# Two weight groups split on VectorE, squares of x on two engines, an earlier first split, and last sums by tokens, in a one-layer diffusion trunk on one core

## The chip, the cores and the metric

The kernel runs on one core of a Trainium2 chip. The metric is device microseconds of one execution; every version gets a median of several runs. A profile is one execution of its own, read with the views of the trace. The engines go by short names: PE is TensorE (PEld its weight loads), DVE VectorE, ACT ScalarE, POOL GpSimd, and SP is SyncE, which only issues transfers. Every engine works through its own instructions in order, and the transfers that SP and POOL issue stand in those engines' order too.

## What is computed

One inference step of a backbone with one trunk layer, over 128 context tokens and 512 latent tokens with 1,024 channels. Cut to what matters here:

```python
def rmsnorm(x, g):
    xf = x.astype(jnp.float32)
    y = xf * lax.rsqrt(jnp.mean(xf * xf, axis=-1, keepdims=True) + EPS)
    return y.astype(x.dtype) * g
...
    sh1, sc1, g1, sh2, sc2, g2 = jnp.split(mod.astype(x.dtype), N_MOD, axis=-1)
    h = rmsnorm(x, p['norm1_g']) * (1 + sc1) + sh1
    proj = jnp.einsum('btd,dc->btc', h, p['w_in']) + p['b_in']
...
    q, k, v, o, i_f, f_f, i_b, f_b, u, ga, gb = jnp.split(proj, offs, axis=-1)
    hA, st_f, st_b = mlstm_bidir(...)          # four heads, forward and backward
    branch_a = jnp.einsum('bte,ed->btd', jax.nn.sigmoid(o) * hA, p['w_proj_a'])
    ua, ub = jnp.split(u, 2, axis=-1)
    z = dwconv1d(ua * jax.nn.sigmoid(ub), p['conv_dw_w'], p['conv_dw_b'])   # 31 taps
    z = jax.nn.silu(layernorm(z, p['conv_ln_g'], p['conv_ln_b']))
    branch_b = jnp.einsum('bte,ed->btd', z, p['w_proj_b'])
    merged = jax.nn.sigmoid(ga) * branch_a + jax.nn.sigmoid(gb) * branch_b
    x = x + g1 * jnp.einsum('btd,de->bte', merged, p['w_out'])
    ...                                        # second norm, gated MLP with a depthwise convolution
    y = rmsnorm(x, p['final_norm_g'])
```

`mod` comes from a linear map of the conditioning vectors. Context tokens see only context tokens.

## The kernel before

**Layout.** Channels lie on the 128 partitions and the 640 tokens are columns, so that x is eight tiles of 128x640. Both token sets go through every matmul together, in two halves of 320 columns.

**Weights in three products.** The weights come in 138 groups of eight 128x128 blocks (512 KB). A group is loaded by SP into a staging buffer `wst` (three of them) and split into a high half `wh` in a format that PE runs at full rate, and a low half `wl`, the remainder; there are three buffers for each half. The activations are split alike (`hh`, `hl`), and a product is the sum of three: `hh`·`wh`, `hl`·`wh` and `hh`·`wl`. A group of the input projection is so 8 blocks x 3 products x 2 column halves = 48 matmuls.

**Two ways to the low half** (`prep`, line 474). ACT always writes `wh`. For most groups DVE then subtracts: `wl = wst - wh`. For groups in the set `TWICE` (lines 162 to 164) ACT writes a second, negated copy into `wl`, and POOL issues a transfer that adds the group from HBM onto it once more (the accumulating DMA `wl<-in_w`), which leaves the same remainder. DVE has no part in these. `TWICE` holds input groups from the seventh on, except those that the value projections hold, and most groups of the MLP. The groups around the change are u2 (11), u6 (12), u3 (13), u7 (14), k2 (15), q2 (16), k3 (17), q3 (18), then the values v1 (19 and 20): u is the input of the gated convolution, k and q are keys and queries of a head.

**What orders the work.** The kernel is emitted once by a planner, `_Order` (line 187): each operation gets an estimated duration; side tasks are generators (`spawn`, line 288) that are advanced when the estimated time of PE has come to their inputs (`until`, line 305), and convolution taps are background work (`later`, `fill`) put in where DVE's estimate leaves a hole. `force` (line 275) runs a task to its end at once. The planner's estimates only set the order; on the chip every engine waits for what it needs.

**The start.** `colsum_into` (line 665) sums squares over the partitions: four matmuls of a 128x32 block of ones, each over a quarter of the tokens (160 columns), so that the sums lie as 128x160, each quarter repeated over 32 partitions. The squares of the eight x tiles are all on ACT (lines 725 to 732), with the tanh of the conditioning and the change to the square root's function table after the fourth. `rstd` (line 683) makes 1/sqrt with one Newton step: a square root on ACT (`rsy`), then on DVE `rsv`, a reciprocal, and three small products (`rst`, `rst`, `rsy`). `bcast` lays the result out as one row per token for all partitions. `ada1` (line 757) makes the modulation from eight columns of weights (`adst`): matmuls with `sc_pad`, a copy `mrow` on ACT, a transposing matmul, then `mods` and `a` on DVE. `first_h` multiplies x by the norm and applies the modulation, giving `hh` and `hl`. `prep(0)` splits the first weight group; it is called before `ada1` starts, and its operations go out when the planner's time for them has come.

**The masks.** In the middle, the scan's decay matrices `E` are filled: `spread` (line 1109) broadcasts rows with SP's transfers, then POOL adds a mask from HBM with accumulating transfers `E<-in_mask`, three per pair of heads. In POOL's order they stand among the accumulating transfers of the weights and the small memsets of the padded `glu` tiles for the convolution.

**The convolution.** `glu` is the gated product of a u pair (128x656 with its padding). ACT makes a first tap (`z<-glu,cols`), and DVE adds the others in 0.8 us each, `z<-glu,cols,z`, in a chain per 128 channels (m = 0 to 3).

**The end.** The last down projection is done in two parts of tokens, 384 and 256 (`PARTS`, line 1747). For each, `final` (line 1749) waits for the squares, which are added on DVE into two tiles, sums them with `colsum_into`, calls `rstd`, lays the row out with `bcast_part`, multiplies and stores. The second part's chain is the last work in the program.

Of the kernel before, what the change touches and what calls it, by code (L numbers as in the profile page):

```python
# [12 lines left out]
AF = mybir.ActivationFunctionType  # L13
ALU = mybir.AluOpType

P = 128
# [4 lines left out]
T = NCTX + NLAT  # L21
# [55 lines left out]
TL = 384  # L77
# [71 lines left out]
GB = 8  # L149
BLOCKS, HELD, PAIRS = _blocks()  # L150
# [10 lines left out]

_IN = [_g for _g in range(NGRP) if BLOCKS[_g * GB][0] in ("q", "k", "v", "u", "o")]
TWICE = set(_IN[6:]) - {_g + 3 for _g in _IN if HELD.get(_g)}
TWICE |= {_g for _g in range(NGRP) if all(nm == "up" and m % NF >= 2 or nm[:2] == "dn" for nm, k, m in BLOCKS[_g * GB:_g * GB + GB])}
UNIT_AT = {_u: _i for _i, _u in enumerate(UNITS)}

# [196 lines left out]
def tile_trunk(  # L363
# [17 lines left out]
    od = _Order()  # L381
    V, S, G, PE, Q, GQ = (_Timed(e, od, k) for e, k in ((nc.vector, "V"), (nc.scalar, "S"), (nc.gpsimd, "G"),
                                                        (nc.tensor, "PE"), (nc.sync, "Q"), (nc.gpsimd, "R")))
# [19 lines left out]
    first, last = ExitStack(), ctx.enter_context(ExitStack())  # L403
    adp = first.enter_context(tc.tile_pool(name="adp", bufs=2 * NAD1))

    def A(shape, dt=F32, name="a"):
        return ap.tile(shape, dt, tag="A", name=name)
# [18 lines left out]
    def ps():  # L426
        return od.ring("ps", pools["ps"].tile([P, 512], F32, tag="ps", name="ps"), pools["nps"])
# [2 lines left out]
        return t[:, 0:T].rearrange("p (h n) -> p h n", h=2)  # L430

    HALF = [slice(0, TH), slice(TH, T)]


    cols = cp.tile([P, NCOLS], F32, name="cols")
    sel = cp.tile([P, NSEL], F32, name="sel")
    ident = sel[:, 0:128]
# [15 lines left out]
    lines = {}  # L453
# [17 lines left out]
    def wtile(tag):  # L471
        return od.ring(tag, (wf[0] if tag == "wf" else wp).tile([P, GB * P], F32R, tag=tag, name=tag), CAPS[tag])

    def prep(g, tags=("wh", "wl")):


        if g in ready or g >= NGRP:
            return
        load(g)
        src = stage.pop(g)  # L480
        tag_of["c", g, 0] = tags
        hi, lo = wtile(tags[0]), wtile(tags[1])

        def parts():
            yield from od.until(src)
            S.activation(hi, src, AF.Copy)
            if g in TWICE:
                S.activation(lo, src, AF.Copy, scale=-1.0)
                live.pop(g)
                GQ.dma_start(lo, w_d[g], accum_op=ALU.add)  # L490
                return
            yield
            V.tensor_sub(lo, src, hi.bitcast(F32))
            live.pop(g)

        ready[g] = (hi, lo)
        lines[g] = od.spawn(parts())
# [137 lines left out]
    def mtile(mat, m, ks, xs, pt=None, first=True, last=True):  # L635
        pt = mm_ps() if pt is None else pt
        outs = [(bank(pt, h), HALF[h]) for h in range(2)]
        for i, k in enumerate(ks):
# [3 lines left out]
    def views(pt, t, rows=slice(0, P)):  # L642
# [3 lines left out]
        if isinstance(pt, tuple):  # L646
            return [(bank(pt, h)[rows], t[:, HALF[h]]) for h in range(2)]
        return [(pt[rows, :, 0:TH], halves(t))]
# [10 lines left out]
    ones32 = cp.tile([P, 32], F32, name="ones32")  # L659
    V.memset(ones32, 1.0)  # L660
    epsc = cp.tile([P, 1], F32, name="epsc")
    V.memset(epsc, EPS)
    bgrp = T // 4

    def colsum_into(pc, tile_, n, first, last):
# [4 lines left out]
    def bcast(r, n):  # L670
        out = []
        for h in range(2):
            pt = ps()
            for j in range(2):
                g = 2 * h + j
                PE.matmul(pt[:, j * n:(j + 1) * n], lhsT=sel[:, 256 + g:257 + g].to_broadcast([P, P]), rhs=r,
                          start=True, stop=True)
            out.append(pt[:, 0:2 * n])
        return out

    def rstd(src, w, scale, name):

# [17 lines left out]
    x = []  # L700
    for j in range(KD):
        t = A([P, T], name="x")
# [21 lines left out]
    pc = ps()  # L724
    for j in range(KD):
        sq = A([P, T], name="sq")
        S.activation(sq, x[j], AF.Square)
        if j == 3:
            th = small([P, 16], "th")
            S.activation(th, colr("c"), AF.Tanh, scale=0.5)  # L730
            sqrt_table()
        colsum_into(pc, sq, bgrp, j == 0, j == KD - 1)
# [11 lines left out]
    for nm in ("b_ua", "b_ub", "b_o", "mlstm_g", "ln_g", "ln_b", "b_ga", "b_gb"):  # L744
        a, b = _COLS[nm]
# [2 lines left out]
        o += b - a  # L748

    r1 = rstd(pc[:, 0:bgrp], bgrp, 1.0 / D, "rs")  # L750
    prep(0)

    def hcol(name, i):
        return halfc[:, HC[name] + i:HC[name] + i + 1]
# [31 lines left out]
    def first_h(j):  # L786
        while not rbs:
            yield
        if j == 0:
            for h in range(2):  # L790
                V.tensor_mul(x[j][:, HALF[h]], x[j][:, HALF[h]], rb[h])
        else:
# [13 lines left out]
    t_ada = od.spawn(ada1())  # L806
    while not mrows:
        od.finish_one()
    rb = bcast(r1, bgrp)
    t = A([P, T], name="rbs")  # L810
    for h in range(2):
        S.activation(t[:, HALF[h]], rb[h], AF.Copy)
    rbs.append(t)
# [130 lines left out]
    for p in range(2):  # L944
        for c in range(NCH):
            t = vp.tile([P, 2, P1], F32, tag="v", name="va")
# [437 lines left out]
    for i, (nm, m) in enumerate(BRANCH):  # L1384
# [9 lines left out]
        else:  # L1394
# [4 lines left out]
            a, b = sgt.pop(("ga", m)), sgt.pop(("gb", m))  # L1399
# [33 lines left out]
    def sums_in(sums, adds, n):  # L1433

        while not all(t[2] for t in adds):
            yield
        pc = ps()
        for i in range(2):
            yield from od.until(sums[i])
            colsum_into(pc, sums[i], n, i == 0, i == 1)  # L1440
        return pc[:, 0:n]

    def bcast_part(r):
        pt = ps()
        n = r.shape[1]
        for g in range(4):
            PE.matmul(pt[:, g * n:(g + 1) * n], lhsT=sel[:, 256 + g:257 + g].to_broadcast([P, P]), rhs=r,
                      start=True, stop=True)
        return pt[:, 0:4 * n]
# [35 lines left out]
    def norm2_part(h, j, rb):  # L1485
        s = HALF[h]
        t, hh = hf[j][:, h, :], h2[j, h]
# [39 lines left out]
    for h in range(2):  # L1527
        sums, adds = [], []
        mat, s = ("woA", "woB")[h], HALF[h]
        pts = [mhalf(mat, m, range(KD - 1), mg, s, last=False) for m in range(2 if h == 0 else 0)]  # L1530
        for m in range(8):
            if m < len(pts):
                pt = mhalf(mat, m, [KD - 1], mg[KD - 1:], s, pt=pts[m], first=False)
            else:
                pt = mhalf(mat, m, range(KD), mg, s)
# [6 lines left out]
    for i in range(2):  # L1542
        t = A([P, TF], name=f"gbuf{i}")
# [200 lines left out]

    ks = LASTF

    PARTS = [slice(0, TL), slice(TL, T)]

    def final(h, sums, adds):
        s = PARTS[h]  # L1750
        n = (s.stop - s.start) // 4
        pc = yield from sums_in(sums, adds, n)
        r3 = rstd(pc, n, 1.0 / D, "rs")
        yield
        yield from od.until(r3)
        rb = bcast_part(r3)
        if h == 0:
            for j in range(KD):
                V.scalar_tensor_tensor(x2[j][:, s], x2[j][:, s], col("final_g", j), rb, op0=ALU.mult, op1=ALU.mult)
                Q.dma_start(yT[j, :, s], x2[j][:, s])  # L1760
                yield
            return
        for j in range(0, KD, 2):
            t = A([P, 2, 4 * n], name="yo")
            for i in range(2):
                V.scalar_tensor_tensor(t[:, i, :], x2[j + i][:, s], col("final_g", j + i), rb,
                                       op0=ALU.mult, op1=ALU.mult)
            Q.dma_start(yT[j:j + 2, :, s].rearrange("j p n -> p j n"), t)
# [3 lines left out]
    for h in range(2):  # L1772
        mat, s = ("dnA", "dnB")[h], PARTS[h]
        sums, adds = [], []
        npre = NPRE if h == 0 else 0
        pts = [dn(mhalf, mat, m, ks[:-1], s, last=False) for m in range(npre)]
        for m in range(8):
# [3 lines left out]
            if m < npre:  # L1781
                pt = dn(mhalf, mat, m, ks[-1:], s, pt=pts[m], first=False)
            else:
                pt = dn(mhalf, mat, m, ks, s)
# [136 lines left out]
```

## Time and profile before

| | us |
|---|---|
| three runs | 949.36, 950.96, 951.27 |
| median | 950.96 |
| the profiled execution | 950.29 |
| its span (first to last instruction) | 948.5 |
| PE busy in the span | 914.2 (96%) |
| DVE busy | 742.1 (78%) |
| ACT busy | 531.6 (56%) |
| POOL busy | 130.6 (14%) |

In a time line, a row has its start in the span, its length, the engine, the line, the operation, the tile it writes, an arrow, what it reads, sizes, and how many instructions the row holds; the square brackets behind it give how long the engine was idle before, and what ended that. A row of windows has the start and end of the stretch, its length, the busy time and count of PE, PEld, DVE, ACT and POOL, then the clock granted to PE (1 is full), the share of the DMA engines and GB/s. A row of the transfers has the tile, the issuing queue, the count, the size and the median us from issue to landing. Every tile operation goes through one helper, so that all rows carry line 182 (183 in the changed kernel, which has one line more above it); rows are told apart by their tiles.

### The profile page before, as it was taken

To read this page: it belongs to the slowest core of one execution; us is meant where nothing else is said; L and a number is where in the kernel's file an instruction comes from. 1 tells how busy PE (TensorE), PEld (TensorE's weight loads), DVE (VectorE), ACT (ScalarE), POOL (GpSimd) and SP (SyncE) were. 2 spreads that over 40 slices of the span, in tenths; PEclk is the share of its full clock that TensorE was granted. 3 is DMA by queue.
4 is the path that set the end of the run, shared out by engine and by line. 5 is a ranking of instruction groups with operands and counts; after the bars stand their busy time and mean duration, and the time that the engine had idled before them with its cause. 6 is when DMAs were issued, how large, how long until landed. Compare 5 with 4: busy or idle time off the path is not lost.

```text
span 948.5 us, 16981 instructions
## 1 busy us (share of the span) xinstructions
PE 914.2 (96%) x6456; PEld 893.0 (94%) x6456; DVE 742.1 (78%) x1540; ACT 531.6 (56%) x995; POOL 130.6 (14%) x181
## 2 busy tenths in 40 slices
PE   5999997999999999999999999999999999999995
PEld 2899997999999999999999999999999999999995
DVE  3829777887857988889788996877778877878666
ACT  5564575267758222223478766646765666666662
POOL 0001212000000000000000112222222222222210
PEclk9999999899999999999999999999999999999998
DMA  9638939543215646667544769887888889889975
GB/s 356 264 121 170 241 96 264 129 101 89 79 46 166 202 154 196 205 204 257 172 156 133 166 143 201 169 179 169 183 171 183 174 172 183 176 175 185 206 166 150
DMA packets 65954, 164.90 MB, mean 174 GB/s; under 512 B 6864, under 2 KB 15824, under 8 KB 65872
## 3 DMA queue, kind: packets, MB, share of 16 engines
q1 hardware_dynamic: 41360, 113.20, 37.0%
q0 software_dynamic: 24512, 50.60, 31.5%
q8 instruction: 51, 0.84, 0.4%
q14 instruction: 31, 0.25, 0.1%
HBM read 151.39 MB, written 3.48 MB: 163 GB/s over the span
## 4 chain that ended last, share of the span: by engine, by line
PE 83%; DMA 6%; DVE 4%; ACT 3%; issue 2%; SPq 0%; DVEq 0%; POOLq 0%; POOL 0%; ACTq 0%
PE mm L182 64%; PE ps L182 19%; DMA wl<-in_w 2%; DMA E<-in_mask 1%; DMA rowM<-M 1%; DMA out_ocst<-cs 1%; DMA x<-in_xT 1%; ACT L182 1%; DMA E<-rowM 1%; DVE x L182 0%; ACT z L182 0%; SPq L182 0%; DVE wl L182 0%; DMA cb<-in_crow 0%; DVE bc L182 0%
## 5 line engine op out<-in xcount | busy, mean ns | idle before, releaser
L182 ACT ACTIVATE wh<-wst 128x1024 fp32r<-128x1024 f32 (+1 forms) x114 | 114.1, 1007 | 99.2 <-PE mm L182 85.9
L182 DVE SCALAR_TENSOR_TENSOR acc<-gbuf,cols,acc 128x455 f32<-128x455 f32 (+2 forms) x176 | 129.7, 740 | 14.8 <-ACT acc L182 12.4
L182 PE MATMUL mm<-hh,wl 128*128 128x320 f32 (+2 forms) x576 | 134.8, 313 | 5.6 <-DMA wl<-in_w 5.6
L182 PE MATMUL mm<-hh,wh 128*128 128x320 f32 (+2 forms) x576 | 134.3, 312 | 2.9 <-ACT hh L182 1.6
L182 PE MATMUL mm<-hl,wh 128*128 128x320 f32 (+2 forms) x576 | 134.9, 313 | 0.0
L182 DVE SCALAR_TENSOR_TENSOR z<-glu,cols,z 128x641 f32<-128x641 f32 (+14 forms) x120 | 102.4, 887 | 22.6 <-ACT z L182 21.6
L182 POOL DMA_DIRECT2D wl<-in_w x69 | 60.9, 883 | 390.3 <-ACT wl L182 225.5
L182 PEld LDWEIGHTS mm<-hh,wl 128*128 128x128 f32 x576 | 97.0, 190 | 7.1 <-DMA wl<-in_w 5.9
L182 PEld LDWEIGHTS mm<-hh,wh 128*128 128x128 f32 x576 | 97.7, 190 | 4.8 <-ACT hh L182 2.1
L182 PEld LDWEIGHTS mm<-hl,wh 128*128 128x128 f32 x576 | 97.1, 190 | 1.8 <-issue 1.3
L182 PE MATMUL mm<-h,wh 128*128 128x320 f32 x452 | 85.5, 310 | 1.4 <-ACT h L182 0.8
L182 DVE SCALAR_TENSOR_TENSOR junk<-ad,cb 128x512 bf16<-128x512 f32 x128 | 82.0, 685 | 0.0
L182 DVE TENSOR_TENSOR wl<-wst,wh 128x1024 fp32r<-128x1024 f32 x55 | 67.1, 1221 | 17.2 <-ACT wh L182 17.1
L182 PE MATMUL mm<-al,wh 128*128 128x320 f32 (+2 forms) x336 | 80.5, 309 | 0.0
L182 PE MATMUL mm<-ah,wh 128*128 128x320 f32 (+2 forms) x336 | 80.3, 309 | 0.0
L182 PE MATMUL mm<-ah,wl 128*128 128x320 f32 (+2 forms) x336 | 80.3, 308 | 0.0
L182 ACT ACTIVATE wl<-wst 128x1024 fp32r<-128x1024 f32 (+1 forms) x91 | 74.3, 840 | 4.7 <-PE mm L182 4.7
L182 PEld LDWEIGHTS mm<-h,wh 128*128 128x128 f32 x452 | 71.2, 188 | 2.7 <-DVE h L182 1.2
L182 PE MATMUL mm<-h,wl 128*128 128x320 f32 x364 | 73.1, 309 | 0.3 <-DMA wl<-in_w 0.3
L182 DVE SCALAR_TENSOR_TENSOR x<-mm,mods,x 128x128 f32<-128x128 f32 (+1 forms) x168 | 63.7, 433 | 8.1 <-PE mm L182 7.5
L182 PEld LDWEIGHTS mm<-h,wl 128*128 128x128 f32 x364 | 58.5, 188 | 0.6 <-DMA wl<-in_w 0.6
L182 PEld LDWEIGHTS mm<-ah,wh 128*128 128x128 f32 x336 | 57.2, 188 | 0.1
(249 smaller groups left out, 1930.6 us busy)
## 6 DMA issues: line engine op xcount, KB each, us to landing
wst<-in_w SPq DMA_DIRECT2D x138, 512.0 KB, 4.5
wl<-in_w POOLq DMA_DIRECT2D x47, 512.0 KB, 7.2
ad<-in_ada SPq DMA_DIRECT2D x64, 256.0 KB, 3.1
adst<-in_ada SPq DMA_DIRECT2D x16, 512.0 KB, 10.2
wf<-in_w POOLq DMA_DIRECT2D x23, 256.0 KB, 5.0
wh<-sf POOLq DMA_DIRECT2D x22, 256.0 KB, 5.3
wl<-in_w POOLq DMA_DIRECT2D x22, 256.0 KB, 6.0
x<-in_xT SPq DMA_DIRECT2D x16, 320.0 KB, 5.8
```

The lines of the kernel that those rows point to most:

```text
L182: return fn(*args, **kw)
```

## The change

It has four parts.

1. Groups k2 and q2 are taken out of `TWICE`: their low halves come from DVE's subtraction, and ACT's second copy and POOL's transfer for them go away.
2. The squares of x tiles 3, 4, 5 and 7 are made on DVE, those of 0, 1, 2 and 6 on ACT; the tanh and the table change come after the third tile's step.
3. `prep(0)` is called after the first `mrow`, doesn't ask the planner to wait for the load, and is forced out at once, ahead of the broadcast of the norm.
4. In the last norm's second part (256 tokens) the sums go by tokens: the squares are the weights and one column of ones is moved, so that the sums lie as 128x2, one token per partition; `rstd` works on 128x2; and `token_rows` broadcasts that column as the weight and moves an identity matrix, which gives the rows for all partitions. It is also written so that the first of the two tiles of squares can be summed before the last square is done.

```diff
 TWICE = set(_IN[6:]) - {_g + 3 for _g in _IN if HELD.get(_g)}
+TWICE -= {_g for _g in _IN if BLOCKS[_g * GB][0] in ("k", "q") and BLOCKS[_g * GB][2] == 2}
...
-    def prep(g, tags=("wh", "wl")):
+    def prep(g, tags=("wh", "wl"), wait=True):
...
-            yield from od.until(src)
+            if wait:
+                yield from od.until(src)
             S.activation(hi, src, AF.Copy)
...
+    def token_sums(pc, tile_, w, first, last):
+
+        n = w // P
+        for c in range(n):
+            PE.matmul(pc[:, c:c + 1], lhsT=tile_[:, c * P:(c + 1) * P], rhs=ones32[:, 0:1], start=first and c == 0,
+                      stop=last and c == n - 1)
+
+    def token_rows(r, a, b):
+
+        pt = ps()
+        for c in range(a, b):
+            PE.matmul(pt[:, (c - a) * P:(c - a + 1) * P], lhsT=r[:, c:c + 1].to_broadcast([P, P]), rhs=ident,
+                      start=True, stop=True)
+        return pt[:, 0:(b - a) * P]
...
         sq = A([P, T], name="sq")
-        S.activation(sq, x[j], AF.Square)
-        if j == 3:
+        if j in (3, 4, 5, 7):
+            V.tensor_mul(sq, x[j], x[j])
+        else:
+            S.activation(sq, x[j], AF.Square)
+        if j == 2:
...
     r1 = rstd(pc[:, 0:bgrp], bgrp, 1.0 / D, "rs")
-    prep(0)
...
         od.finish_one()
+    prep(0, wait=False)
+    od.force(lines[0])
     rb = bcast(r1, bgrp)
...
-        n = (s.stop - s.start) // 4
-        pc = yield from sums_in(sums, adds, n)
+        if h == 0:
+            n = (s.stop - s.start) // 4
+            pc = yield from sums_in(sums, adds, n)
+        else:
+            n = (s.stop - s.start) // P
+            while not all(t[2] for t in adds[:-1]):
+                yield
+            yield from od.until(sums[0])
+            pc = ps()
+            token_sums(pc, sums[0], n * P, True, False)
+            while not adds[-1][2]:
+                yield
+            yield from od.until(sums[1])
+            token_sums(pc, sums[1], n * P, False, True)
+            pc = pc[:, 0:n]
         r3 = rstd(pc, n, 1.0 / D, "rs")
         yield
         yield from od.until(r3)
-        rb = bcast_part(r3)
+        rb = bcast_part(r3) if h == 0 else token_rows(r3, 0, n)
```

Since the planner sets the order, the change also moves instructions. On DVE at the start, the sequence from the first norm's `rsv` on stands like this in the kernel before (a row is an operation with its output, inputs and shape, and how many of it follow one another):

```order
L182 TENSOR_SCALAR rsv<-ps 128x160
L182 RECIPROCAL rsy<-rsy 128x160
L182 TENSOR_TENSOR rst<-rsy 128x160
L182 SCALAR_TENSOR_TENSOR rst<-rst,rsv 128x160
L182 SCALAR_TENSOR_TENSOR rsy<-rst,rsy 128x160
L182 TENSOR_SCALAR mods<-ps,cols 128x2
L182 TENSOR_SCALAR a_213<-ps,sc1p,cols 128x2
L182 TENSOR_TENSOR x<-x,ps 128x320 x2
L182 TENSOR_TENSOR wl<-wst,wh 128x1024
```

In the changed kernel the same place on DVE reads:

```order
L183 RECIPROCAL rsy<-rsy 128x160
L183 TENSOR_TENSOR rst<-rsy 128x160
L183 SCALAR_TENSOR_TENSOR rst<-rst,rsv 128x160
L183 SCALAR_TENSOR_TENSOR rsy<-rst,rsy 128x160
L183 TENSOR_TENSOR wl<-wst,wh 128x1024
L183 TENSOR_SCALAR mods<-ps,cols 128x2
L183 TENSOR_SCALAR a_211<-ps,sc1p,cols 128x2
L183 TENSOR_TENSOR x<-x,ps 128x320 x2
```

The split of group 0 has moved from behind the first multiplies by the norm to between the norm's last product and `mods`. Further up, DVE's four squares (`sq<-x`) stand ahead of its small preparations of the modulation; on ACT the copy `wh` of group 0 stands ahead of `rbs`, where it stood behind.

On DVE in the middle, at the gating product `glu` of the third channel block (m = 2) and the convolution taps `z` around it, the kernel before has:

```order
L182 SCALAR_TENSOR_TENSOR z<-glu,cols,z 128x651
L182 SCALAR_TENSOR_TENSOR glu<-gt,gy 128x128
L182 SCALAR_TENSOR_TENSOR glu<-gt,gy 128x512
L182 SCALAR_TENSOR_TENSOR z<-glu,cols,z 128x652
L182 SCALAR_TENSOR_TENSOR z<-glu,cols,z 128x653
L182 SCALAR_TENSOR_TENSOR z<-glu,cols,z 128x641
L182 SCALAR_TENSOR_TENSOR z<-glu,cols,z 128x654
L182 SCALAR_TENSOR_TENSOR z<-glu,cols,z 128x642
L182 SCALAR_TENSOR_TENSOR z<-glu,cols,z 128x655
```

In the changed kernel the same place has the two new splits, k2's first and then q2's:

```order
L183 SCALAR_TENSOR_TENSOR glu<-gt,gy 128x128
L183 SCALAR_TENSOR_TENSOR glu<-gt,gy 128x512
L183 TENSOR_TENSOR wl<-wst,wh 128x1024
L183 SCALAR_TENSOR_TENSOR z<-glu,cols,z 128x652
L183 SCALAR_TENSOR_TENSOR z<-glu,cols,z 128x653
L183 SCALAR_TENSOR_TENSOR z<-glu,cols,z 128x641
L183 SCALAR_TENSOR_TENSOR z<-glu,cols,z 128x654
L183 SCALAR_TENSOR_TENSOR z<-glu,cols,z 128x642
L183 TENSOR_TENSOR wl<-wst,wh 128x1024
L183 SCALAR_TENSOR_TENSOR z<-glu,cols,z 128x655
```

One split stands right behind `glu`, the other behind five more taps (of these, 652 and 653 end the chain of the second channel block and 641 begins the third's). Some 45 rows on, the first value rows `va<-mm,vb` stand two taps earlier in the fourth block's chain than before.

On POOL, the same stretch, from the masks `E` of the second pair of heads on, reads in the kernel before:

```order
L182 DMA E<-in_mask 128x4x128
L182 DMA E_1676<-in_mask 128x8x128
L182 DMA E_1684<-in_mask 128x8x128
L182 MEMSET glu 128x15
L182 MEMSET glu 128x1
L182 DMA wl<-in_w 128x1024 x2
L182 MEMSET glu 128x15
L182 MEMSET glu 128x1
L182 DMA wl<-in_w 128x1024 x7
```

In the changed kernel:

```order
L183 DMA E<-in_mask 128x4x128
L183 DMA E_1676<-in_mask 128x8x128
L183 DMA E_1684<-in_mask 128x8x128
L183 MEMSET glu 128x15
L183 MEMSET glu 128x1
L183 MEMSET glu 128x15
L183 MEMSET glu 128x1
L183 DMA wl<-in_w 128x1024 x7
```

The two weight transfers between the memsets, those of k2 and q2, are gone, and the first that follows the masks is k3's. On PE the last rows of the program are now two sums of two 128x1 matmuls and two 128x128 matmuls for the broadcast, where two sums of four 32x64 matmuls and four of 128x64 stood.

More of the change, by code (lines that the diff above doesn't have):

```diff
@@ L432, in tile_trunk @@
     HALF = [slice(0, TH), slice(TH, T)]
+    PARTS = [slice(0, TL), slice(TL, T)]
     cols = cp.tile([P, NCOLS], F32, name="cols")
@@ L1745, in tile_trunk @@
     ks = LASTF
-    PARTS = [slice(0, TL), slice(TL, T)]
     def final(h, sums, adds):
         s = PARTS[h]
-        n = (s.stop - s.start) // 4
-        pc = yield from sums_in(sums, adds, n)
+        if h == 0:
[13 more added lines that the diff above has]
+            pc = pc[:, 0:n]
         r3 = rstd(pc, n, 1.0 / D, "rs")
@@ L1763, in final @@
         for j in range(0, KD, 2):
-            t = A([P, 2, 4 * n], name="yo")
+            t = A([P, 2, n * P], name="yo")
             for i in range(2):
```

## The prediction

> **What bounds the kernel now.** I read the page first (busy time by engine), then PE's waits, then the chain of waits around the longest of them, the time lines of the engines feeding it, and last the start and the end of the span, which the diff also touches.
>
> ```profile
> PE   914.2 (96%) x6456; PEld 893.0 (94%) x6456; DVE 742.1 (78%) x1540; ACT 531.6 (56%) x995; POOL 130.6 (14%) x181
> ...
> PE mm L182 <- DMA wl<-in_w: 6.0, 2, 5.6
> ```
>
> TensorE (PE) is busy for 96% of the 948.5 us span, and no matmul of the trunk goes away. So only PE's gaps, and stretches at a lowered clock, can be won. The largest is a wait of 5.6 us for `wl<-in_w`, the low half of a weight group finished by an accumulating DMA. The chain and PE's time line there:
>
> ```profile
> 153.45 0.08 POOL glu L182
> 153.53 12.78 DMA wl<-in_w
> ...
> 160.26 0.46 PE L182 MATMUL mm<-hl,wh 128*128 128x320 f32 x2
> ...
> 166.35 0.90 PE L182 MATMUL mm<-hh,wl 128*128 128x320 f32 x2 [5.63 <-DMA wl<-in_w]
> ...
> 171.31 0.46 PE L182 MATMUL mm<-hh,wl 128*128 128x320 f32 x2
> 171.60 0.46 PE L182 MATMUL mm<-hh,wh 128*128 128x320 f32 x2
> ...
> 166.00:171.30 5.30, 4.95 (x18) 4.95 (x19) 5.30 (x7) 0.00 (x0) 0.00 (x0) 0.50 0.92 230
> ```
>
> The group is k2 (the third head's key weights). Two matmul halves are one row, and rows follow each other every 0.29 us (171.31 to 171.60). The next row was due at 160.26 + 0.29 = 160.55 and came at 166.35: 5.8 us lost. Then the granted clock is 0.50 (the figure behind the five busy times), and nine rows take 171.31 − 166.35 = 4.96 us where nine at 0.293 take 2.64: 2.3 us more. The stall costs 5.8 + 2.3 = 8.1 us.
>
> Why k2's low half is late stands on GpSimd's (POOL's) and ScalarE's (ACT's) lines:
>
> ```profile
> 148.51 1.56 POOL L182 DMA_DIRECT2D E<-in_mask  x1 [7.14 <-DVE z L182]
> 152.56 1.55 POOL L182 DMA_DIRECT2D E<-in_mask  x1 [2.49 <-DMA E<-rowM]
> ...
> 153.53 1.59 POOL L182 DMA_DIRECT2D wl<-in_w  x1
> ...
> 163.15 0.86 POOL L182 DMA_DIRECT2D wl<-in_w  x1 [4.03 <-ACT wl L182]
> ...
> 147.16 1.05 ACT L182 ACTIVATE wh<-wst 128x1024 fp32r<-128x1024 f32 x1
> ...
> 154.31 0.93 ACT L182 ACTIVATE z<-glu,cols 128x656 f32<-128x656 f32 x1 [5.15 <-POOL glu L182]
> ...
> 155.82 1.04 ACT L182 ACTIVATE wh<-wst 128x1024 fp32r<-128x1024 f32 x1
> ```
>
> k2's high half was ready at 147.16 + 1.05 = 148.2. Its accumulating DMA stands behind two mask transfers in POOL's order, is issued at 153.53, and lands 12.8 us later, beside them.
>
> **k2 and q2 split on VectorE (DVE).** Its split, and the two stretches in which the new ones stand:
>
> ```profile
> L182 DVE TENSOR_TENSOR wl<-wst,wh 128x1024 fp32r<-128x1024 f32 x55 | 67.1, 1221 | 17.2 <-ACT wh L182 17.1
> ...
> 155.27 9.75 DVE L182 SCALAR_TENSOR_TENSOR z<-glu,cols,z 128x641 f32<-128x641 f32 x12 [4.52 <-ACT z L182]
> ...
> 165.75 19.55 DVE L182 SCALAR_TENSOR_TENSOR z<-glu,cols,z 128x647 f32<-128x647 f32 x24
> 192.92 10.52 DVE L182 SCALAR_TENSOR_TENSOR z<-glu,cols,z 128x641 f32<-128x641 f32 x13 [7.62 <-ACT z L182]
> ```
>
> k2's split stands right after the gating product `glu`, ahead of DVE's 4.52 us of idle before 155.27; its input is there at 148.2. DVE's idle began at 155.27 − 4.52 = 150.75, behind two taps that now follow the split, so `glu` ended near 149.1 and 1.22 us of split ends by 150.3, ten microseconds before PE needs it, and costs nothing. q2's stands three taps (0.81 us each) into the chain starting at 155.27, so at 157.7, after its `wh` (155.82 + 1.04 = 156.9), and ends at 158.9; k2 now runs from 160.0 to 167.0, and q2's low half is needed only then. Without DVE's idle time k2's split would still have ten microseconds. So the stall goes: −8.1.
>
> What is late next? q2's split moves the end of DVE's chain from 165.75 + 19.55 = 185.3 to 186.5. The next 13 taps waited 7.62 us for an ACT operation that stands behind a PE result and so comes 8.1 earlier: 192.92 − 8.1 = 184.8. They begin at 186.5, 1.7 late; but the value rows `va`, which PE reads and which stood right behind them, move two taps (1.6 us) ahead. I give back 0.2, and 1.8 at most, if PE were to wait for all of DVE's lag. The two ACT copies and two transfers that go take nothing off the path by themselves.
>
> The next accumulating DMA is k3's, issued at 163.15 behind an ACT copy that waits for a buffer, which does not change:
>
> ```profile
> wl<-in_w POOLq DMA_DIRECT2D x1, 512.0 KB, 9.5
> wl<-in_w POOLq DMA_DIRECT2D x1, 512.0 KB, 13.2
> ```
>
> The first row is k3's own landing (issues of 163.1 to 163.2 us): 172.65, with q2's transfer still beside it, which goes. PE will need it two rows into k3: 160.0 + 2 × 7.05 + 0.6 = 174.7 (a group is 24 rows of 0.293). Margin 2.0 us. The second row is the longest landing of such a transfer near mask transfers (group u2, issued at 105.1).
>
> [...]
>
> **The start** (squares on two engines; group 0 split earlier):
>
> ```profile
> 9.77 2.60 ACT L182 ACTIVATE sq<-x 128x640 f32<-128x640 f32 x4
> L182 DVE TENSOR_TENSOR x<-x,rbs 128x640 f32<-128x640 f32 x7 | 5.7, 816 | 0.0
> x<-in_xT SPq DMA_DIRECT2D x1, 320.0 KB, 6.6
> wst<-in_w SPq DMA_DIRECT2D x1, 512.0 KB, 7.4
> 15.81 0.32 DVE L182 SCALAR_TENSOR_TENSOR rsy<-rst,rsy 128x160 f32<-128x160 f32 x1
> 17.04 0.98 ACT L182 ACTIVATE rbs<-ps 128x320 f32<-128x320 f32 x2 [1.68 <-PE ps L182]
> 18.02 0.22 DVE L182 TENSOR_SCALAR mods<-ps,cols 128x2 f32<-128x2 f32 x1 [1.89 <-PE ps L182]
> ```
>
> ACT's last square ends at 12.37. The last x tile (third row, issue in 4.7 to 4.8 us) lands at 4.73 + 6.6 = 11.3; a two-input DVE product over 128x640 takes 0.82 (second row), so the last square ends at 12.2, the arrival bounding it: −0.2. DVE's small preparations for the modulation now stand behind its squares; what hides them is PE's sum of the last square and ACT's square root behind it, and without that cover they would cost a part of the bound below. The split of group 0 needs its load (fourth row, issue in 8.1 to 8.2 us): 15.5. Copy 15.55 to 16.6, before `rbs` at 17.04; split 16.65 to 17.9, in DVE's idle between `rsy` (ends 16.13) and `mods` (18.02). It was behind the multiplies by the norm and nothing on PE waited for its end, so moving it gains nothing; I take −0.15 for the start, somewhat under the 0.2. The cover is thin: `mods` stands behind the split, and every microsecond of lateness of that load beyond 0.1 would be paid by the first matmul. Bounds: −0.3, and +2.8 if the load took the longest median of the issues then:
>
> ```profile
> adst<-in_ada SPq DMA_DIRECT2D x16, 512.0 KB, 10.2
> ```
>
> **The end** (last norm of 256 tokens by tokens):
>
> ```profile
> 937.72 0.32 PE L182 MATMUL ps<-sq,ones 128*32 128x64 f32 x8 [0.43 <-ACT sq L182]
> 938.59 0.54 DVE L182 RECIPROCAL rsy<-rsy 128x64 f32<-128x64 f32 x1
> 939.69 0.23 DVE L182 SCALAR_TENSOR_TENSOR rsy<-rst,rsy 128x64 f32<-128x64 f32 x1
> 940.06 1.94 PE L182 MATMUL ps<-rsy,sel 128*128 128x64 f32 x8 [2.02 <-DVE rsy L182]
> ...
> 17.38 0.61 PE L182 MATMUL ps<-sel,mrow 128*128 128x128 f32 x4
> 145.64 0.21 DVE L182 RECIPROCAL hry<-hry 128x10 f32<-128x10 f32 x1
> 146.29 0.17 DVE L182 SCALAR_TENSOR_TENSOR hry<-hrt,hry 128x10 f32<-128x10 f32 x1
> ```
>
> Here everything is a chain, so every term counts. Each fp32 matmul is two passes in the trace. The second sum: four passes with 128 weight columns instead of eight with 32; by the 128x128 passes at full clock (0.61 / 4 = 0.15) 0.61 instead of 0.32: +0.3, and at half clock +0.9. The reciprocal and three small products now have 2 columns instead of 64: from 938.59 to 939.92 was 1.33; the same chain on 10 columns took 145.64 to 146.46 = 0.82: −0.5. The broadcast: four passes of 128 columns for eight of 64; at the half-clock tempo of the 940.06 row (1.94 / 8 = 0.24) −0.97, at twice 0.15 −0.7, at full clock −1.3. Sum: 0.3 − 0.5 − 0.97 = −1.2, between −0.3 (0.9 − 0.5 − 0.7) and −1.5.
>
> **The sum.** −8.1 + 0.2 − 0.15 − 1.2 = −9.25. The profiled execution took 950.29 us (span 948.5 plus 1.8 around it), 0.67 below the median of the runs shown, 950.96. So 950.29 − 9.25 = 941.04, and as a median 941.7.
>
> **Rivals.**
>
> *The wait moves to the next transfer.* If k3's transfer took the 13.2 us of u2's, it would land at 176.35, 1.7 after PE wants it, with a lowered clock behind it of at most the 2.3 above: 4.0 given back, 945.7. It decides from a landing of 11.5 us on. For it: such transfers near masks took 12.8 and 13.2. Against: this one took 9.5 with q2's beside it, and the masks have landed when it is issued. 14%.
>
> *Slower: VectorE becomes the pace.* PE's results come 8.1 earlier, DVE has 2.44 more to do, and its idle time from here through the scan is limited:
>
> ```profile
> 165.00:300.00 135.00, 131.96 (x976) 128.77 (x977) 103.43 (x214) 80.84 (x179) 5.15 (x6) 0.98 0.39 98
> ```
>
> DVE (third busy figure) is idle for 135 − 103.4 = 31.6. If more than 31.6 − 8.1 − 2.44 = 21 of that were idle time that its own chains need (results passed to and fro with ACT), the 8.1 would be waited out again for DVE's results, the splits added, and a second lowered stretch of 2.3 with it: 2.44 + 2.3 − 0.15 − 1.2 = +3.4, that is 954.4. Against: the largest single idle, the 7.62 ahead of 192.92, hangs on PE's progress and not on DVE's chain. 6%.
>
> *It doesn't do what it says.* The split is emitted early but PE at 160.6 still finds something late (the high half's copy, a staging buffer), so the middle gains nothing: −1.35, 949.6. Against: `wh` was ready at 148.2. 7%.
>
> **How the numbers follow.** Forecast 73%, moved wait 14%, not as said 7%, slower 6%. A measurement here can tell about 0.2%, 1.9 us, from no change. The forecast and the moved wait are faster (0.87), the one not as said is the same (0.07), VectorE's pace slower (0.06). The range: down to −8.1 − 0.3 − 1.5 = −9.9 on the median (941.1) less the 1.6 by which the lowest run shown lies under the median: 939.5. Up: the moved wait's 945.7 with the scatter of 0.3 over the median shown: 946.0; this also holds DVE's lag of 1.8 and the start's bound of 2.8, one at a time.
>
> **What would show it.** Right: no PE wait for `wl<-in_w` near 160, rows 0.29 apart through k2, clock 1.00 from 160 to 176, k3's low half landed before 174.7; DVE's split ending before 151 and 159; the last square by 12.2, the first trunk matmul near 20.4; the end from the last square's sum to `yo` 1.2 shorter than 942.04 − 937.72 = 4.3. Wrong: PE waiting for `wl` in k3, for `va` after 195, or `mods` starting after 18.1 at the start. If the stall goes and the span falls by less than 6, a new wait between 174 and 300 has taken its place.

## The result, and the profile after

The changed kernel takes 942.0 us (median of 4 runs, 940.93 to 942.33), the kernel before in the same runs 950.25 (4 runs). The ratio is 0.9911, with a 95% interval of 0.9894 to 0.9928. The forecast was 941.7. The profiled execution took 941.9 us with a span of 940.1, against 950.29 and 948.5: 8.4 us less.

PE's waits in the profile after, the longest groups (in total, times, longest):

```profile
PE ps L183 <- ACT sq L183: 5.3, 3, 4.3
PE mm L183 <- DMA wl<-in_w: 3.2, 3, 1.5
...
PE mm L183 <- DVE va L183: 1.1, 1, 1.1
```

There are still waits for `wl<-in_w`, but none is near 160, and the longest is 1.5. The windows of the place where the stall stood:

```profile
160.00:166.00 6.00, 6.00 (x43) 6.00 (x43) 6.00 (x10) 2.69 (x3) 0.89 (x1) 1.00 0.70 182
166.00:171.30 5.30, 5.30 (x38) 5.30 (x38) 5.30 (x7) 2.69 (x3) 0.68 (x1) 1.00 0.64 129
171.30:176.00 4.70, 4.70 (x34) 4.70 (x33) 4.70 (x7) 1.34 (x2) 0.18 (x1) 1.00 0.94 197
```

PE is busy all the time, at a granted clock of 1.00. The time line of DVE shows the two new splits, and the one of POOL what is left between the masks and k3's transfer:

```profile
149.37 1.22 DVE L183 TENSOR_TENSOR wl<-wst,wh 128x1024 fp32r<-128x1024 f32 x1
...
158.18 1.22 DVE L183 TENSOR_TENSOR wl<-wst,wh 128x1024 fp32r<-128x1024 f32 x1
...
164.96 30.79 DVE L183 SCALAR_TENSOR_TENSOR z<-glu,cols,z 128x653 f32<-128x653 f32 x38
195.66 0.42 DVE L183 TENSOR_TENSOR va<-mm,vb 128x256 f32<-128x256 f32 x1
```

```profile
153.06 1.55 POOL L183 DMA_DIRECT2D E<-in_mask  x1 [2.47 <-DMA E<-rowM]
153.94 0.90 POOL L183 MEMSET glu<- 128x15 f32 x4
163.60 0.89 POOL L183 DMA_DIRECT2D wl<-in_w  x1 [8.75 <-DVE z L183]
```

The splits end at 150.6 and 159.4 (forecast 150.3 and 158.9). The second thus ends after the 159 that the prediction named as a sign of being right, still 8.6 us before PE reads its result (168.02). The 38 taps from 164.96 now run without the idle of 7.62 that stood among them, and `va` comes at 195.66 (195.4 by the forecast's sum). k3's transfer landed 7.0 us after its issue, at 170.6, over 4 us before PE wants it (175.04).

The start went another way. Rows of ACT, DVE and PE there:

```profile
11.02 0.83 DVE L183 TENSOR_TENSOR sq<-x 128x640 f32<-128x640 f32 x1 [0.77 <-DMA x<-in_xT]
...
15.39 1.05 ACT L183 ACTIVATE wh<-wst 128x1024 fp32r<-128x1024 f32 x1
...
15.68 2.50 PE L183 MATMUL ps<-rsy,sel 128*128 128x160 f32 x8 [0.63 <-DVE rsy L183]
16.48 1.23 DVE L183 TENSOR_TENSOR wl<-wst,wh 128x1024 fp32r<-128x1024 f32 x1 [0.85 <-ACT wh L183]
...
17.97 1.06 PE L183 MATMUL ps<-sel,mrow 128*128 128x128 f32 x4
...
19.07 0.22 DVE L183 TENSOR_SCALAR mods<-ps,cols 128x2 f32<-128x2 f32 x1 [1.37 <-PE ps L183]
...
21.97 0.56 PE L183 MATMUL mm<-hh,wh 128*128 128x256 f32 x2 [1.59 <-ACT hh L183]
```

The last square ends at 11.85, the split ends at 17.7, and neither holds anything up. But the broadcast of the norm takes 2.50 us where it took 1.35, and the modulation's product 1.06 where it took 0.61: PE works at about half its tempo. The first trunk matmul comes at 21.97, 1.4 later than before, and `mods` starts at 19.07, behind the 18.1 that the prediction named as a sign of being wrong: it waited for PE, though, and not for the load of group 0. The views print a granted clock of 1.00 here for both profiles, but they print 1.00 also where a trace holds no record of the clock. The first record starts at 14.27 in the profile before, ahead of its broadcast at 16.19, and at 19.73 in this one, behind the broadcast at 15.68. What the clock is without a record is told here by the durations; a profile further down prints 0.50 at that time.

The end, on PE:

```profile
931.03 0.61 PE L183 MATMUL ps<-ones,sq 128*128 128x1 f32 x4 [0.17 <-ACT sq L183]
...
932.94 0.68 PE L183 MATMUL ps<-sel,rsy 128*128 128x128 f32 x4 [1.30 <-DVE rsy L183]
```

The second sum takes 0.3 longer, the chain on DVE is shorter, and the broadcast takes 0.68 instead of 1.94.

To see where time went in all versions I cut every profile at the same instructions of PE: the broadcast of the first norm, the first trunk matmul, the wait for ACT's `gt` near 60, the wait for `va` near 113, the first `ps<-q,k` behind the stall, `mm<-zh` near 336, `mm<-h` behind the `h` wait near 513, `mm<-ah` near 911, the last square's sum, and the end of the span. Each figure is the time from one cut to the next.

| profile | broadcast starts | to first matmul | to gt | to va | to q,k | to zh | to h | to ah | to last sum | to end |
|---|---|---|---|---|---|---|---|---|---|---|
| before | 16.19 | 4.38 | 39.57 | 52.55 | 84.57 | 138.84 | 176.79 | 398.60 | 26.23 | 10.78 |
| changed | 15.68 | 6.29 | 39.60 | 53.10 | 74.89 | 138.36 | 176.88 | 400.00 | 26.23 | 9.07 |
| changed, again | 16.10 | 6.81 | 39.58 | 52.99 | 76.43 | 138.40 | 176.90 | 398.88 | 26.22 | 9.59 |
| groups alone | 15.81 | 6.17 | 39.54 | 53.46 | 75.06 | 137.74 | 176.80 | 398.61 | 26.21 | 10.80 |
| squares alone | 16.12 | 5.49 | 42.34 | 53.74 | 82.25 | 138.45 | 176.64 | 398.55 | 26.24 | 10.78 |
| first split alone | 16.25 | 4.38 | 39.52 | 53.33 | 83.30 | 139.26 | 176.85 | 399.10 | 26.15 | 10.76 |
| last norm alone | 16.32 | 4.38 | 39.57 | 53.70 | 84.27 | 139.29 | 176.80 | 398.23 | 26.23 | 9.61 |
| without squares | 16.07 | 4.38 | 39.54 | 53.27 | 76.50 | 138.83 | 176.87 | 398.60 | 26.21 | 9.53 |
| without first split | 16.36 | 5.49 | 42.70 | 52.82 | 76.04 | 138.09 | 176.75 | 398.55 | 26.27 | 9.53 |
| without both | 16.35 | 6.04 | 39.57 | 52.73 | 76.38 | 137.78 | 176.85 | 398.18 | 26.25 | 9.57 |

### The profile page after: what moved, and what is told of

It reads as the page before. It is cut to its first block, busy times and chain, and to the rows that moved or that the text cites. A ratio compares the mean times of both kernels' runs of the same rounds, so it can differ in the third digit from the quotient of the medians.

```text
span 940.1 us, 16953 instructions
## 1 busy us (share of the span) xinstructions
PE 912.7 (97%) x6444; PEld 890.2 (95%) x6444; DVE 747.8 (80%) x1546; ACT 526.7 (56%) x989; POOL 128.9 (14%) x179
## 4 chain that ended last, share of the span: by engine, by line
PE 83%; DMA 6%; DVE 5%; issue 2%; ACT 2%; SPq 1%; DVEq 0%; POOLq 0%; ACTq 0%
PE mm L183 64%; PE ps L183 19%; DMA wl<-in_w 2%; DMA E<-in_mask 1%; DMA rowM<-M 1%; DMA wf<-sf 1%; DMA x<-in_xT 1%; SPq L183 1%; DMA E<-rowM 1%; DVE acc L183 0%; DVE x L183 0%; DVE wl L183 0%; DMA cb<-in_crow 0%; DVE sq L183 0%; DVE bc L183 0%
## 5 line engine op out<-in xcount | busy, mean ns | idle before, releaser
L183 POOL DMA_DIRECT2D wl<-in_w x67 | 57.8, 863 | 387.0 <-ACT wl L183 194.4
L183 DVE TENSOR_TENSOR wl<-wst,wh 128x1024 fp32r<-128x1024 f32 x57 | 69.6, 1221 | 17.9 <-ACT wh L183 17.9
L183 ACT ACTIVATE wl<-wst 128x1024 fp32r<-128x1024 f32 (+1 forms) x89 | 72.1, 835 | 4.7 <-PE mm L183 4.7
```

Source lines behind the costliest of these rows:

```text
L183: return fn(*args, **kw)
```

## The experiments

The kernel before ran beside every version on the same chip; its median was 949.94 beside the first four versions (29 runs), 950.51 beside the next four (11), 951.57 beside the last four (17). Ratios are to those.

**The groups alone, the squares alone, the first split alone, the last norm alone.** Each puts one part of the change into the kernel before.

```diff
+TWICE -= {_g for _g in _IN if BLOCKS[_g * GB][0] in ("k", "q") and BLOCKS[_g * GB][2] == 2}
```

> Only k2 and q2 leave the accumulating route; the start and the end are those of the kernel before. My theory (the stall of 5.8 us and its half-clock rows of 2.3 us go, and only DVE's lag of 0.2 comes back): no PE wait near 160, first trunk matmul at 20.6, time 8 us under the kernel before, with at most 1.4 us of it returned by a longer wait for a low half near 519, which the changed kernel shows (1.35 us against 0.33). Rival (the changed kernel's whole gain of 8.3 us is the sum of this and other terms that cancel by chance: the middle is worth under 6.5): time 6.5 us under or less.

Measured: 941.28, ratio 0.9899 (0.9880 to 0.9918), about 9 us (8.7 between the medians). The stage with the stall falls from 84.57 to 75.06. My theory stands; the longer wait near 519 doesn't appear, so that wait of the changed kernel's profile isn't given back by this part.

The start of this kernel is that of the kernel before, instruction for instruction, and still its profile shows PE's slow tempo:

```profile
15.81 2.50 PE L183 MATMUL ps<-rsy,sel 128*128 128x160 f32 x8 [0.84 <-DVE rsy L183]
```

The slow tempo can so come without any change at the start.

```diff
-        S.activation(sq, x[j], AF.Square)
-        if j == 3:
+        if j in (3, 4, 5, 7):
+            V.tensor_mul(sq, x[j], x[j])
+        else:
+            S.activation(sq, x[j], AF.Square)
+        if j == 2:
```

> Only the squares of x go to two engines. Theory A (the slow tempo of PE's passes between 14 and 19 us of the changed kernel, broadcast 2.50 us against 1.35, comes with the squares' new timing): the broadcast of the first norm takes over 2.2 us, first trunk matmul at 21.5 or later, time 0.5 to 1.5 us over the kernel before. Theory B (it comes with the early split of group 0): broadcast 1.35, first trunk matmul near 20.3, time 0 to 0.3 us under. Theory C (it differs from execution to execution): either picture in the profile, time within 0.7.

Measured: 953.25, ratio 1.0029 (1.0016 to 1.0042), nearly 3 us slower, more than any of the theories gave. The broadcast is slow (2.50), but most of the loss lies behind it, between the first trunk matmul and `gt`: 42.34 against 39.57. PE's first matmul in that profile, and the windows after it:

```profile
21.61 0.56 PE L182 MATMUL mm<-hh,wh 128*128 128x256 f32 x2 [2.14 <-ACT hh L182]
```

```profile
22.00:24.00 2.00, 1.98 (x19) 0.94 (x19) 1.39 (x3) 0.38 (x1) 0.47 (x1) 0.69 1.04 414
24.00:26.00 2.00, 2.00 (x14) 1.33 (x16) 0.73 (x3) 0.00 (x0) 1.54 (x12) 0.50 1.02 404
```

PE had waited 2.14 us for `hh` (1.59 in the kernel before) and ran at a granted clock of 0.69 and 0.50 behind it. What differs there is PE's order. In the kernel before, the second modulation product (`adst`) stands ahead of the first trunk matmuls:

```
ps<-sel,mrow 128x128 x2
ps<-adst,sc_pad 32x256 x8
mm<-hh,wh 128x256
mm<-hh,wh 128x384
```

and with the squares alone behind them:

```
ps<-sel,mrow 128x128 x2
mm<-hh,wh 128x256
mm<-hh,wh 128x384
ps<-adst,sc_pad 32x256 x8
```

so that PE has nothing to do until `hh` is there. Of the 2.77 us that the stage up to `gt` takes longer, about 1.1 is this product itself (1.07 in the kernel before), which now lies in this stage and not ahead of it; the rest fits the stretch of 0.50, which the windows (0.69 over 22 to 24, 0.50 over 24 to 26, 0.96 over 26 to 28) put at about 22.8 to 26.2: by my estimate, 3.4 us at half the tempo lose 1.7.

```diff
-    prep(0)
...
+    prep(0, wait=False)
+    od.force(lines[0])
```

> Only group 0 is split earlier. Theory A (the slow tempo comes with the squares): broadcast 1.35 us, first trunk matmul near 20.6, time within 0.3 us of the kernel before. Theory B (the split ahead of the norm's broadcast copy on ACT and of the modulation on DVE holds the start): first trunk matmul at 21.5 or later, time 0.5 to 1.5 us over. Theory C: either picture in the profile, time within 0.7.

Measured: 950.26, ratio 0.9995 (0.9982 to 1.0008); broadcast 1.35, first matmul at 20.63. Theory B (the early split holds the start) fell.

```diff
-        rb = bcast_part(r3)
+        rb = bcast_part(r3) if h == 0 else token_rows(r3, 0, n)
```

(with `token_sums` in place of `colsum_into` for this part, as in the change)

> Only the last norm's second part goes by tokens. My theory after seeing the changed kernel (chain from the last square to the first output multiply 1.7 us shorter, as the broadcast runs at full clock, four passes in 0.68 us): time 1.7 us under the kernel before, all of it after the last square, broadcast 0.7 us at a granted clock of 1.00. Rival (as in the prediction, the broadcast runs at half clock and the changed kernel's profile was a lucky one): broadcast near 1.0 us at clock 0.50, time 1.2 us under.

Measured: 947.77, ratio 0.9981 (0.9968 to 0.9995), 1.8 us. In its profile the end takes 9.61 instead of 10.78: 1.2, not the changed kernel's 1.7. The broadcast took 1.19 there, at a granted clock of 0.50 (940.69 to 941.89), so the rival (the changed kernel's first profile was a lucky one) holds; the interval of the times, 0.5 to 3.0 us, can't tell 1.2 from 1.7.

**The change without its squares, without its first split, without both, and once more.** These tell whether the squares cost the same in the company of the other parts. The edits are the diffs above, undone.

> The changed kernel with all squares on ACT again (early split, groups and last norm stay). Theory P (the squares cost 2.8 us when alone because the planner then issues the second adaLN product ahead of the first group's matmuls on PE; the forced early split puts PE's order back, so that in the changed kernel the squares cost nothing): time within 0.7 us of the changed kernel run beside it. Theory Q (the squares cost the same wherever they stand): 2 to 3 us under the changed kernel.

> The changed kernel with group 0 split at its old place (squares on two engines stay). Theory P: PE's order of the start is that of the kernel with the squares alone; time 2 to 3 us over the changed kernel run beside it, the loss between the first trunk matmul and 62 us of the span, where granted clock falls to 0.5. Theory Q: within 0.7 us of it.

> Both parts at the start undone, groups and last norm kept. Theory P: the pair is worth 0.2 us or less, time within 0.7 us of the changed kernel. Theory Q: 2 to 3 us under it, near 938.7, as the two single runs would add up to (0.9899 x 0.9981 of the kernel before).

> The changed kernel once more, unaltered, for its profile and as the measure of its neighbours. Theory C (PE's tempo between 14 and 19 us differs from execution to execution, as the kernel with the groups alone showed the slow one with the start of the kernel before): broadcast of the first norm either 1.35 or 2.50 us, first trunk matmul either near 20.5 or near 22.0; time near 941.5. Theory A (the squares bring it): 2.50 again.

Measured, in this order: 941.41 (ratio 0.9908, 0.9886 to 0.9930), 944.58 (0.9939, 0.9916 to 0.9961), 941.75 (0.9910, 0.9887 to 0.9934), 942.63 (0.9921, 0.9897 to 0.9945). The intervals overlap, so the stages decide: without the first split the stage up to `gt` is 42.70, as with the squares alone, and its windows show the same fall:

```profile
22.00:24.00 2.00, 1.69 (x19) 0.85 (x20) 1.63 (x4) 0.38 (x1) 0.22 (x1) 0.93 1.04 414
24.00:26.00 2.00, 2.00 (x14) 1.55 (x18) 0.49 (x3) 0.00 (x0) 1.55 (x12) 0.50 1.04 408
26.00:28.00 2.00, 2.00 (x21) 1.00 (x14) 0.65 (x1) 0.62 (x2) 0.38 (x1) 0.72 1.02 406
```

With the first split forced, squares or not, it is 39.5 to 39.6. That is theory P: the squares' loss is one of PE's order, and the forced split puts the order right (its text on record has the direction of the move turned round: the product goes behind the matmuls, not ahead). What the two together bring is nothing that these runs can tell; the changed kernel without them is as fast or a little faster.

The broadcast's tempo, in the kernel without squares and in the changed one again:

```profile
16.07 1.35 PE L183 MATMUL ps<-rsy,sel 128*128 128x160 f32 x8 [1.25 <-DVE rsy L183]
```

```profile
16.10 2.50 PE L183 MATMUL ps<-rsy,sel 128*128 128x160 f32 x8 [0.61 <-DVE rsy L183]
```

**k2 alone and q2 alone split on VectorE**, the rest as in the change:

```diff
-TWICE -= {_g for _g in _IN if BLOCKS[_g * GB][0] in ("k", "q") and BLOCKS[_g * GB][2] == 2}
+TWICE -= {_g for _g in _IN if BLOCKS[_g * GB][0] == "k" and BLOCKS[_g * GB][2] == 2}
```

> The changed kernel with k2 split on VectorE but q2 back on the accumulating route. My theory (what stalls PE is a transfer queued behind the masks, so the wait moves to the next group that still takes that route): no wait at k2, q2's transfer issued at 154 to 158 and landing 11 to 13 us later, against 167.6 where PE wants it: between no wait at all (issued at once, landing 167) and 2 to 3 us with a lowered clock behind; time 0 to 4 us over the changed kernel. Rival (k2 alone was the trouble, q2's split is superfluous): q2's low half lands before 167, no wait, time within 0.7 us of the changed kernel.

> The changed kernel with q2 split on VectorE but k2 back on the accumulating route. My theory: k2's transfer is still issued near 153.5 behind the masks and PE waits for it, 5.6 us less at most 2 that a neighbour transfer fewer saves, with the lowered clock behind; time 5 to 8 us over the changed kernel. Rival (the two transfers together made each other late): the wait at k2 shrinks under 2 us, time at most 3 over.

Measured: k2 alone 942.29 (ratio 0.9922, 0.9901 to 0.9943), as the changed kernel; q2 alone 950.31 (0.9996, 0.9981 to 1.0012), no faster than the kernel before. With k2 alone, q2's transfer is issued at 159.33, behind an ACT copy and not behind the masks:

```profile
159.33 0.89 POOL L183 DMA_DIRECT2D wl<-in_w  x1 [3.84 <-ACT wl L183]
```

```profile
wl<-in_w POOLq DMA_DIRECT2D x1, 512.0 KB, 7.7
```

It lands at 167.0, before PE wants it (168.66), and PE has no wait there; the rival holds and q2's split is superfluous. In the kernel before, the transfers of POOL's queue landed one behind the other in the order of their issue: two masks at 159.6 and 163.9, k2 at 166.3, q2 at 169.8, k3 at 172.6. Without k2's, q2's is the next to land behind the masks (160.5 and 163.3 in this profile). With q2 alone, the chain of waits reads as in the kernel before:

```profile
154.67 11.84 DMA wl<-in_w
...
166.55 13.52 PE mm L183 x81
```

PE waits 4.87 for it. k2's split is the whole gain of the middle, by removing one transfer that stood behind the masks.

**Idle PE kept busy at the start**, in the changed kernel and in the one without squares:

```diff
+    pw = ps()
+    wone = cp.tile([P, 160], F32, name="wone")
+    V._eng.memset(wone, 1.0)
+
+    def busy(n):
+        for i in range(n):
+            g = i % 4
+            PE._eng.matmul(pw[32 * g:32 * g + 32, 0:160], lhsT=ones32, rhs=wone, start=True, stop=True,
+                           tile_position=(0, 32 * g))
+
+    busy(20)
     for j in range(KD):
...
+        if j < 4:
+            busy(2)
```

> The changed kernel with idle PE kept busy before and between the first squares' sums: 28 more matmuls on a tile of ones, whose result is read by nobody. Theory W (PE's tempo up to 19 us depends on how busy PE was before; in the kernels with squares on two engines the broadcast took 2.50 us in 4 profiles of 4, with them on ACT in 2 of 6): broadcast 1.35 us, first trunk matmul near 20.3, time 1 to 2 us under the changed kernel. Rival (phase alone decides, whatever PE does): broadcast 1.35 or 2.50, time within 0.7 us of the changed kernel.

> The same extra matmuls in the changed kernel with all squares on ACT. Theory W: broadcast 1.35 us, first trunk matmul near 20.4, time 0.3 to 1 us under the same kernel without them (941.4), the lowest of all versions together with the one before. Rival (phase alone): broadcast 1.35 or 2.50, time as without them.

Measured: 940.69 (ratio 0.9898, 0.9878 to 0.9918) and 940.04 (0.9890, 0.9870 to 0.9910), the lowest medians of all; yet both broadcasts took 2.50 and the first matmuls came at 22.30 and 21.97. Theory W fell: the times are lower, but not by what I meant, and the intervals touch those of the kernels without the extra matmuls. In both profiles PE's wait for `va` near 113 is short (none, and 0.31 us); whether the extra matmuls bring that isn't shown. In the first of the two, PE's sums ran faster for a while (0.48 us for eight passes) and slower again ahead of the broadcast (0.76 for the same), and the windows print a granted clock of 1.00 and then of 0.50 there:

```profile
11.63 0.48 PE L183 MATMUL ps<-sq,ones 128*32 128x160 f32 x8 [0.26 <-ACT sq L183]
12.56 0.76 PE L183 MATMUL ps<-sq,ones 128*32 128x160 f32 x8 [0.44 <-DVE sq L183]
...
16.61 2.50 PE L183 MATMUL ps<-rsy,sel 128*128 128x160 f32 x8
```

```profile
5.70:12.40 6.70, 3.59 (x62) 1.56 (x54) 3.17 (x4) 3.17 (x5) 0.00 (x0) 1.00 1.02 396
12.50:19.30 6.80, 5.55 (x34) 3.32 (x35) 4.74 (x19) 2.31 (x5) 0.14 (x2) 0.50 1.03 412
```

The slow broadcast of 2.50 is thus one at a granted clock of 0.50 in the first of these profiles. The second has the same turn in its durations: eight passes of a sum take 0.48 at 8.10, sixteen of the modulation product 2.26 at 14.15 and 1.07 at 19.32. In the profiles of the kernel before and of the changed one the record starts with 1.00, at 14.27 ahead of the fast broadcast and at 19.73 behind the slow one. As the other slow broadcasts took the same 2.50, I read them as half clock too; that is an inference from their durations.

The groups alone have the same instructions at the start as the kernel before, and their broadcast took 2.50 against 1.35. So the same start can show both tempos. What sets the time at which the clock comes to full isn't shown.

Over all 14 profiles the broadcast is slow in 7 of 7 with squares on two engines and in 3 of 7 with all on ACT. This doesn't show that the squares bring it, as the slow broadcast came without them too; whether they make the slow start more frequent stays open.

## Why the prediction was right, point by point

*The stall in the middle (−8.1, and 0.2 given back): right.* Stage for stage, with the clock behind the `va` wait lowered in both, 84.57 (before) and 84.27 (last norm alone) stand against 76.50, 76.38 and 76.43: −8.0. With that clock at 1.00 in both, 82.25 and 83.30 stand against 74.89, 75.06 and 76.04: −7.5. The changed kernel's own profile shows −9.7, as it stood on the other side of this clock than the profile before; the 1.7 beyond −8.0 is no work of the change, since two executions of the changed kernel itself differ so (74.89 and 76.43). DVE's lag cost nothing visible: PE had no wait for `va` after 195.

*q2's part: not needed.* I argued that the wait would move to the next transfer, and for q2 it doesn't: it isn't issued right behind the masks once k2's is gone, and lands 1.7 us before PE wants it. The rival of the moved wait is gone with it: wherever k2 is split on VectorE, k3's transfer lands 3.4 to 5.2 us before PE wants it.

*The start (−0.15): the sign was wrong.* The squares ended as worked out and the load was there in time. What failed is a step that I took without a word: that PE's broadcast and products would run at the tempo of the profile before. They ran at about half of it (2.50 and 1.06 us against 1.35 and 0.61), the record of a clock of 1.00 starts only at 19.73 and not at 14.27, and the first matmul came 1.4 later, inside the bound of 2.8 that I had drawn for another cause. The groups alone show that this can come with the old start as well, so it is a matter of the execution and not shown to be one of the change. That the squares by themselves would turn PE's order round was also not in the forecast; the forced split hides it.

*The end (−1.2): right for most executions, in part by luck.* Five profiles of the table with the new end took 9.53 to 9.61, 1.2 under 10.78. The changed kernel's first profile took 9.07, since its broadcast ran at a granted clock of 1.00; once more, at 0.50, the same row reads:

```profile
934.21 1.19 PE L183 MATMUL ps<-sel,rsy 128*128 128x128 f32 x4 [1.30 <-DVE rsy L183]
```

The terms of this sum were off in opposite directions. From the start of the second sum to the broadcast it is 1.91 instead of 2.34 us, −0.4 where I had +0.3 − 0.5 = −0.2; the broadcast at half clock takes 1.19 instead of 1.94, −0.75 where I had −0.97.

*The sum* of −9.25 became −8.4 between the two profiles: +1.4 at the start (0.5 earlier to the broadcast, 1.9 longer to the first matmul), +0.6 up to `va`, −9.7, −0.4 up to `h`, +1.4 in the MLP, −1.7 at the end. The 1.4 in the MLP, most of it one wait of 1.35 for `wl<-in_w` near 519 that was 0.33 before, belongs to this execution: the nine others of the table take 398.2 to 399.1 in that stage, the same kernel once more 398.9 (q2 alone, which is not in the table, took 399.4 with a wait of 1.13 there); the 0.6 is a wait of 1.46 near 78, which versions without the groups' change show too (1.14 to 1.53). So the total came out near the forecast partly because terms that belong to single executions cancelled.

## What to carry to other kernels

Here a transfer was late by what stood ahead of it in its issuing queue: k2's landed 12.8 us after its issue, behind two masks that landed at 159.6 and 163.9, and q2's 7.7 us after its own once k2's was gone. Take the first one behind such a block off its queue, by a few instructions on an engine that idles there, and measure whether the next ones need it at all: here one group of two did the whole work. Where a planner sets the order, try each part of a change alone, since a harmless part can turn the order of another engine; and cut several profiles at the same instructions before a term is put down to the change.

## What the runs showed of the hardware that I had not expected

PE's granted clock was lowered behind some waits of about 2 us. At one place, the wait for `va` near 113 to 117, the next 5 us ran at 1.00 in eight profiles and at 0.66 or 0.67 in five (in the fourteenth there is no wait). Behind waits of 0.31 (without squares, with the extra matmuls), 1.08 (the changed kernel), 1.29 (k2 alone) and 1.84 us (q2 alone) it was 1.00, behind that of 2.15 us in the kernel before 0.66. The stage took 74.89 us with 1.00 and 76.43 with 0.66 in the changed kernel's two profiles, about 1.5 more. The windows behind the wait of 1.84 (q2 alone) and that of 2.15 (before):

```profile
115.00:120.00 5.00, 4.95 (x42) 4.96 (x43) 5.00 (x9) 4.35 (x15) 0.00 (x0) 1.00 0.79 138
```

```profile
112.60:117.60 5.00, 4.91 (x28) 4.91 (x29) 4.81 (x9) 4.30 (x15) 0.00 (x0) 0.66 0.93 155
```

In the kernel before, the record has 0.50 for 3.41 us here (113.26 to 116.67) and for 6.83 us at the wait for k2 (164.46 to 171.29). At the start, the waits for `hh` of 1.59 us in the kernel before, the changed kernel, the changed kernel again and the one without squares left the clock at 1.00; behind the 2.14 us in the two kernels with the other order of PE (squares alone, without first split) the windows show 0.50. The 0.55 us more of waiting, and the stretch at 0.50 behind it, came with 2.1 us more from the broadcast to `gt` in the kernel with the squares alone than in the one with the groups alone, which has the same slow broadcast (47.83 against 45.71).

At the end, nearly the same waits of 0.85, 0.17 and 1.30 us stand around the small matmuls of the sums, and the broadcast behind them took 1.19 or 1.20 us in six profiles (at 0.50 in four of them: last norm alone, without both, k2 alone, and the changed kernel, again), 1.07 and 1.09 in two (without squares and without first split, 0.56 and 0.54 over the 1.2 us from its start), 0.86 in one (q2 alone), and 0.68 in the changed kernel's first profile, where the clock was 1.00 and fell at 934.50, behind it. So the waits alone don't tell the clock, and these runs don't show what does.
